# Layer 1 of a two-layer decoder: the order in which query and key stacks, weights, the last head and the memory's keys are worked

## The chip, the cores and the metric

One core of a Trainium2 chip. The metric is the device time of one execution of the whole program, in microseconds (us). The engines are TensorE (PE: matmuls; PEld: its weight loads), VectorE (DVE), ScalarE or Activation (ACT), GpSimd (POOL) and SyncE (SP, which issues most DMAs). Each runs its own instructions in order and waits for the others by semaphores.

## What is computed

A decoder of two layers over 1024 positions with 1024 features, in float32. Layer 0 has differential attention with 6 heads, layer 1 stick-breaking attention with 12 heads on keys and values that are projected once from the residual stream; both have a cross-attention into 256 memory tokens, a SiLU gate, an output projection and a residual addition. Layer 1, cut to what the change touches:

```python
h = rms_norm(x, b_norm[j]); proj = h @ b_w_in[j]
q, qm, gate = jnp.split(proj, [SB_W, SB_W + MEM_W], axis=-1)
# stick-breaking, per block of 128 queries
z = q @ k.T * scale
log_beta = log_sigmoid(z); log_1m = where(mask, log_sigmoid(-z), 0.0)
suffix = cumsum(log_1m, reverse=True) - log_1m
o = exp(where(mask, log_beta + suffix, -inf)) @ v
om = memory_attention(qm, mem, ...)
x = x + (concatenate([o, om]) * silu(gate)) @ b_w_out[j]
```

## The kernel before

Every float32 operand of a matmul is split into a high part, rounded by a cast to `F32R`, and a low part, the difference; a product is three matmuls (`mm3`: high x high, high x low, low x high). So each weight, each `h`, each query and key costs a cast (mostly on Activation) and a subtraction (on VectorE or POOL).

**Order.** TensorE's instructions run in the order in which the Python code emits them. The code builds lists of (cost, function) items; `mixed` and `merge` interleave a main list and a filling list in proportion to their costs, and `spread(a, b)` puts the items of `b` evenly behind the items of `a`. On the other engines and on SP a scheduler orders the instructions by its own estimate of when each can start and by the order in which they are emitted; `urgent()` sets an instruction 150 places further forward. So a change in the lists moves TensorE's work by hand and everything else by way of the scheduler.

**Pools.** PSUM has eight banks: `psc` 3 (scores), `ppj` 2 (all projections, tag `pj`), `ptr` 3 (transposes `tw`, `tb`, `ta`, the attention output `av`, tag `tr`). In SBUF, `wp` has 11 slots (split weights, reloaded outputs `ys`, residuals `res`), `rawp` 4 (weights as they land), `hp` 2 (the split `h` and the split layer output `yh` of one half of 512 tokens).

**Between the layers.** While the output projection of layer 0 for the second half of the tokens (`go1`, 64 items: 8 output blocks of 8) runs, the keys and values of the memory for layer 1 (`kv_products`, 8 items of 12 matmuls, L611 to L632) are merged in. `load_h` then makes `h` of the first half: `norms` (matmul `ms`, L232, then `r_t` on POOL by `rsqrt_pool`, L101), `rows` (L240) and eight urgent pieces. `km` is the memory's statistics, two splits (`prep`) and four turns of the keys (`turn`, matmul `ta`, L389). `plan1` does `norms`, `rows` and the pieces of the second half among the memory's query products `mp[b]` (eight of 8 items); their `nat` is turned by `turn_q` (`tb`, L378).

**A head in layer 1** (`StickUnit`, two of the 12 heads at a time, c = 0 and 1). `take_q` and `take_k` read a projection bank: Activation copies the high parts (L912, L913, L921), VectorE subtracts for the low parts. `S` makes scores, two sigmoids on Activation (L942, L943), a mask on POOL (L947), a scan (L949) and a product `be` on VectorE. `W` transposes `be` (`tw`, L531), splits it into `wT`, multiplies with the values (`av`, L971), and joins the halves: Activation copies `avt` (L980) and VectorE adds `y`. In `run_layer` step `n` has the scores of pair `n` and the `W` of the pair before; the projections of the next head and the gates fill in.

**Weights.** `load_turned` (L140) loads up to three blocks of 128 columns, `load_flat` (L158) one of 256. On the way "act" POOL scales the raw weight in place by the norm's gain, Activation casts it, POOL subtracts.

**The last head.** `out_proj(1, 0)` and `out_proj(1, 1)` give `load0`, `go0`, `load1`, `go1`: loads of the heads' outputs `y` from memory (`ys`, split to `yh`, L1017), and 64 items each, item (m, i) being block t = `order[i]` of output block m, with t = 5, the last head, at the end of each m. `tail` says what of them goes into which step of the last head (B = 48).

```python
items[0:2] = [items[0][:7], items[1][:7], items[0][7:], items[1][7:]]      # out_proj, l = 1, c = 0
tail = {B + 1: load0[:3], B + 2: load0[3:], B + 3: go0[:4], B + 4: go0[4:8] + load1[:3], ...
```

Of the kernel before, what the change touches and what calls it, by code (L numbers as in the profile page):

```python
# [8 lines left out]
F32 = mybir.dt.float32  # L9
F32R = mybir.dt.float32r  # L10
# [29 lines left out]
def trunk(ctx: ExitStack, tc: tile.TileContext, xT, memT, pos, gains, vecs, wA, wAm, wAg, wAo,  # L40
# [99 lines left out]
    def load_turned(ws, i, src, gbase, way="act"):  # L140
# [7 lines left out]
        r3 = raw.rearrange("p (k m) -> p k m", k=n)  # L148
        nc.sync.dma_start(r3, src[:, k0:k0 + n, :])
        tt(G, r3, r3, gn[:, gbase + k0:gbase + k0 + n].unsqueeze(2).broadcast_to([P, n, P]), ALU.mult)  # L150
        w = ws[i] = wp.tile([P, 2, 384], F32R, name="w", tag="w")
        S.copy(w[:, 0, :n * P], raw)  # L152
        tt(G, w[:, 1, :n * P], raw, w[:, 0, :n * P].bitcast(F32), ALU.subtract)
# [4 lines left out]
    def load_flat(ws, kt, src, gbase, st, way="act", last=None):  # L158
# [22 lines left out]
        if way == "vector":  # L181
            S.activation(hi, raw, AF.Copy, scale=g)
            V.scalar_tensor_tensor(lo, raw, g, hi.bitcast(F32), ALU.mult, ALU.subtract)
        else:
            G.tensor_scalar(raw, raw, g, 0.0, ALU.mult, ALU.add)
            S.copy(hi, raw)
            tt(G, lo, raw, hi.bitcast(F32), ALU.subtract)
# [707 lines left out]
    class StickUnit:  # L895
# [9 lines left out]
        def take_q(self, c, ps):  # L905
# [5 lines left out]
            for i, d in enumerate((LOW, HIGH)):  # L911
                S.copy(hi[i][d, :], ps[d, :])  # L912
                S.copy(hi[i][(HIGH, LOW)[i], :], ps[d, :])  # L913
                tt(V, lo[d, i, :], ps[d, :], hi[i][d, :].bitcast(F32), ALU.subtract)
            self.q[c] = hi, lo

        def take_k(self, c, ps):

            k = self.k[c] = kp.tile([P, 2, 512], F32R, name="k", tag="k")
            for i, d in enumerate((LOW, HIGH)):  # L920
                S.copy(k[d, i, :], ps[d, :])  # L921
                tt(V, k[(HIGH, LOW)[i], i, :], ps[d, :], k[d, i, :].bitcast(F32), ALU.subtract)

# [32 lines left out]
        def W(self, bc):  # L956
# [6 lines left out]
            def av(part, k0, k1):  # L963
# [15 lines left out]
                d, s_ = (lo, hi) if c == 0 else (hi, lo)  # L979
                S.copy(tmp[d, :], o[s_, :])  # L980
                tt(V, self.y[d, :], o[d, :], tmp[d, :], ALU.add)
                if c == 1:
# [4 lines left out]
    def value_chunks(p, ws, b):  # L987
# [17 lines left out]
        return [(C256, lambda kt=kt: go(kt)) for kt in range(8)]  # L1005


    def out_proj(l, c, wo):
# [20 lines left out]
        def go(m, i):  # L1029
# [12 lines left out]
            if i == 7:  # L1042
# [9 lines left out]
                else:  # L1052
                    nc.sync.dma_start(out[c, m], res)
        items = [[(C512, lambda m=m, i=i: go(m, i)) for i in range(8)] for m in range(8)]
        if l == 1 and c == 0:
            items[0:2] = [items[0][:7], items[1][:7], items[0][7:], items[1][7:]]
        return ([(0, lambda t=t: load(t)) for t in ((0, 2, 4) if l == 0 else order[:7])],
# [93 lines left out]
    def plan1(mem, hs, after):  # L1151
# [51 lines left out]
        add(-3, mp[0], norms1)  # L1203
        add(-2, mp[1][:7], rows1, p1, mp[1][7:])
        add(-1, spread(mp[2], load_g(7)))
        add(0, mp[3], gate(6, 0))
# [88 lines left out]
    def ends(l, wo):  # L1295
# [12 lines left out]
    first, lg, km, fills, ts, ss = plan1(mems[1], hs1, (n1, r1, p1))  # L1308
    merge(kv, go0 + d0 + go1[:4] + n0 + go1[4:9] + r0 + spread(go1[9:36], p0))
    merge([], spread(go1[36:44], km) + spread(go1[44:57], first + d1[:3]) + spread(go1[57:], lg) + d1[3:])  # L1310
    stick_mask()
    load0, go0 = out_proj(1, 0, wBo)
    load1, go1 = out_proj(1, 1, wBo)
    B = 8 * NH
    late = [(2000, lambda: None)]
    tail = {B + 1: load0[:3], B + 2: load0[3:], B + 3: go0[:4], B + 4: go0[4:8] + load1[:3], B + 5: go0[8:12] + load1[3:5],
            B + 6: go0[12:14] + late + go0[14:20], B + 7: go0[20:30] + load1[5:], B + 8: go0[30:41], B + 9: go0[41:49]}
    run_layer(1, mems[1], (fills, ts, ss), {}, tail)
    merge([], go0[49:] + go1)

# [66 lines left out]
```

## Time and profile before

| | us |
|---|---|
| median of 3 runs | 1349.86 (1347.27 to 1352.76) |
| the profiled execution | 1355.41 |
| its span, first to last instruction | 1353.7 |
| TensorE busy | 1263.8 (93%) |
| VectorE / Activation / POOL busy | 968.3 / 784.3 / 727.9 |
| mean granted TensorE clock | 0.978 |

Layer 0 takes the first 620 us or so, the passage between the layers ends near 745, the six head pairs of layer 1 follow at some 78 us each from 815 on, and the last 92 us are nearly all output projection. In the rows below, times are from the span's start; a group of instructions is given with its busy time, the mean of one in ns, and the idle time before it with what ended it; "busy (x)" is busy time and number of instructions; PEclk is the granted TensorE clock, 1.00 for 2.4 GHz and 0.50 for 1.2.

### The profile page before, as it was taken

To read this page: it belongs to the slowest core of one execution; us is meant where nothing else is said; L and a number is where in the kernel's file an instruction comes from. 1 tells how busy PE (TensorE), PEld (TensorE's weight loads), DVE (VectorE), ACT (ScalarE), POOL (GpSimd) and SP (SyncE) were. 2 spreads that over 40 slices of the span, in tenths; PEclk is the share of its full clock that TensorE was granted. 3 is DMA by queue.
4 is the path that set the end of the run, shared out by engine and by line. 5 is a ranking of instruction groups with operands and counts; after the bars stand their busy time and mean duration, and the time that the engine had idled before them with its cause. 6 is when DMAs were issued, how large, how long until landed. Compare 5 with 4: busy or idle time off the path is not lost.

```text
span 1353.7 us, 22630 instructions
## 1 busy us (share of the span) xinstructions
PE 1263.8 (93%) x7556; PEld 1126.8 (83%) x7556; DVE 968.3 (72%) x2211; ACT 784.3 (58%) x1986; POOL 727.9 (54%) x924
## 2 busy tenths in 40 slices
PE   7799999999999999999888999999899998988998
PEld 6688999898989888887777997789778897876787
DVE  8788777778787876775845645777767777898832
ACT  4566555555555656764645755666646665575631
POOL 7664544636462575945045755655655664455630
PEclk9899999999999999999989999999999999998999
DMA  5010110201011220357540142112120231222453
GB/s 213 24 49 27 39 36 22 58 9 53 23 47 32 74 78 28 124 179 245 176 129 24 34 134 67 45 48 93 52 67 28 75 94 55 69 72 86 131 165 117
DMA packets 75670, 105.65 MB, mean 78 GB/s; under 512 B 8353, under 2 KB 60321, under 8 KB 75297
## 3 DMA queue, kind: packets, MB, share of 16 engines
q1 hardware_dynamic: 75264, 104.05, 24.5%
q8 instruction: 60, 0.98, 0.3%
q14 instruction: 58, 0.47, 0.1%
q10 hardware_dynamic: 288, 0.15, 0.0%
HBM read 82.67 MB, written 21.50 MB: 77 GB/s over the span
## 4 chain that ended last, share of the span: by engine, by line
PE 64%; DVE 14%; POOL 6%; DMA 6%; ACT 5%; issue 5%; POOLq 0%; DVEq 0%; SPq 0%; ACTq 0%
PE pq L416 6%; PE pq L418 5%; PE pq L417 5%; PE tw L531 4%; PE pg L416 4%; PE pg L418 4%; PE pg L417 4%; PE sc L520 3%; PE sc L521 3%; DVE u L949 3%; PE av L971 3%; PE po L417 2%; PE po L416 2%; PE po L418 2%; PE tb L378 2%
## 5 line engine op out<-in xcount | busy, mean ns | idle before, releaser
L94 POOL TENSOR_TENSOR w<-raw,w 128x384 fp32r<-128x384 f32 (+1 forms) x182 | 195.3, 1082 | 32.2 <-ACT w L152 19.0
L416 PE MATMUL pq<-w,h 128*128 128x384 f32 (+1 forms) x448 | 162.0, 362 | 5.6 <-ACT h L223 5.3
L94 DVE TENSOR_TENSOR wT<-tw,wT 128x512 fp32r<-128x512 f32 (+2 forms) x248 | 138.6, 567 | 28.9 <-ACT wT L535 27.1
L949 DVE TENSOR_TENSOR_SCAN u<-u,stick 128x128 f32<-128x128 f32 (+3 forms) x96 | 133.9, 1395 | 32.6 <-ACT u L942 32.2
L418 PE MATMUL pq<-w,h 128*128 128x384 f32 (+1 forms) x448 | 149.7, 334 | 3.4 <-DVE h L224 3.2
L417 PE MATMUL pq<-w,h 128*128 128x384 f32 (+1 forms) x448 | 149.5, 334 | 0.2 <-POOL w L94 0.2
L535 ACT CAST wT<-tw 128x512 fp32r<-128x512 f32 (+2 forms) x248 | 122.3, 500 | 44.5 <-PE tw L531 41.9
L101 POOL TENSOR_TENSOR ss<-ss,mhalf 128x4 f32<-128x4 f32 x68 | 71.0, 1047 | 108.6 <-DVE ss L356 103.4
L947 POOL TENSOR_SCALAR_AFFINE_SELECT be<-be 128x128 f32<-128x128 f32 x96 | 79.0, 825 | 86.3 <-ACT be L943 84.3
L416 PE MATMUL pg<-h,w 128*128 128x512 f32 x256 | 109.4, 427 | 0.1
L818 ACT ACTIVATE e<-sc,nmd 128x512 f32<-128x512 f32 (+2 forms) x144 | 82.5, 579 | 42.9 <-DVE nmd L813 42.2
L416 PE MATMUL po<-yh,w 128*128 128x512 f32 x256 | 105.0, 410 | 2.0 <-DVE res L94 2.0
L418 PE MATMUL pg<-h,w 128*128 128x512 f32 x256 | 102.9, 402 | 1.3 <-POOL w L94 1.3
L417 PE MATMUL pg<-h,w 128*128 128x512 f32 x256 | 102.6, 401 | 0.0
L417 PE MATMUL po<-yh,w 128*128 128x512 f32 x256 | 102.0, 398 | 0.2 <-POOL yh L94 0.2
L94 DVE TENSOR_TENSOR be<-be,u 128x127 f32<-128x127 f32 (+3 forms) x96 | 88.7, 926 | 18.1 <-POOL be L947 13.3
L418 PE MATMUL po<-yh,w 128*128 128x512 f32 x256 | 101.6, 397 | 0.0
L531 PE MATMUL tw<-identR,be 128*128 128x128 f32 x432 | 75.0, 285 | 24.2 <-DVE y L94 12.9
L416 PEld LDWEIGHTS pq<-w,h 128*128 128x128 f32 x448 | 86.0, 192 | 8.4 <-POOL w L122 5.3
L418 PEld LDWEIGHTS pq<-w,h 128*128 128x128 f32 x448 | 85.7, 191 | 4.2 <-DVE h L224 4.2
L417 PEld LDWEIGHTS pq<-w,h 128*128 128x128 f32 x448 | 86.2, 192 | 3.5 <-POOL w L94 0.9
L531 PEld LDWEIGHTS tw<-identR,be 128*128 128x128 f32 x432 | 55.0, 146 | 36.2 <-DVE y L94 14.1
(237 smaller groups left out, 3931.4 us busy)
## 6 DMA issues: line engine op xcount, KB each, us to landing
raw<-in_wA_dram SPq DMA_DIRECT2D x44, 192.0 KB, 2.4
raw<-in_wAo_dram SPq DMA_DIRECT2D x32, 192.0 KB, 2.6
v_dr<-vs SPq DMA_DIRECT2D x48, 128.0 KB, 1.8
v<-v_dr SPq DMA_DIRECT2D x12, 512.0 KB, 3.5
raw<-in_wBo_dram SPq DMA_DIRECT2D x32, 192.0 KB, 2.5
raw<-in_wB_dram SPq DMA_DIRECT2D x36, 128.0 KB, 2.3
raw<-in_wB_dram SPq DMA_DIRECT2D x24, 192.0 KB, 2.4
wkv<-in_wM_dram SPq DMA_DIRECT2D x16, 256.0 KB, 3.1
```

Of the source, the lines that this page charges most:

```text
L94: eng.tensor_tensor(out_, a, b, op)
L101: G.tensor_tensor(t, t, mhalf[:, :n], ALU.pow)
L416: T.matmul(o, a[0], b[0], start=first, stop=False)
L417: T.matmul(o, a[0], b[1], start=False, stop=False)
L418: T.matmul(o, a[1], b[0], start=False, stop=last)
L520: T.matmul(sc[:, :m], qh, k[:, c, :m], start=True, stop=False)
L521: T.matmul(sc[:, :m], ql, k[:, c, :m], start=False, stop=True)
L531: T.transpose(t[:, j * P:(j + 1) * P], w[:, j * P:(j + 1) * P], identF)
L535: S.copy(hi, t3)
L818: S.activation(e[:, o:o + n], st["sc"][j], AF.Exp, bias=nm[:, 0:1], accum_out=st["l"][:, j, c:c + 1])
L947: G.affine_select(out=be[:, L - P:L], in_=be[:, L - P:L], pattern=[[-1, P]], compare_op=ALU.is_gt, fill=0.0, base=0, channel_multiplier=1)
L949: V.tensor_tensor_scan(u[:, 0:L][:, ::-1], u[:, 0:L][:, ::-1], keep["m"][:, 1024 - L:1024][:, ::-1], 1.0, ALU.mult, ALU.max)
```

## The change

1. `load_turned` and `load_flat`, way "act": Activation writes the high part itself with the gain as scale (up to three instructions of 128 columns, or one of 256), ahead of POOL's scaling in place; POOL's subtraction follows.
2. `take_q` and `take_k`: all of Activation's copies are emitted before VectorE's subtractions.
3. `StickUnit.W`: the copy `avt` and the addition `y` are urgent.
4. `out_proj(1, 0)`: the first three output blocks are summed over seven blocks of the input (without t = 5), and the sum is added into the residual at once; the last head's product for these three is done behind the fourth output block, from one more load of three weight blocks (`w5`), with a second addition and the store.
5. `plan1`: `rows` and the pieces of the second half come after three items of `mp[2]` instead of seven of `mp[1]`; the load of gate 7 stands alone.
6. Between the layers: four more items of `go1` before `norms`, six instead of five before `rows`, the pieces over 16 items instead of 27; the memory's statistics before six output items, its split and turns spread over the next 21 items among the loads of the memory's query weights.
7. The tail: output items from step B + 2 on and six more of them within the last head; the second half's loads at B + 8, B + 9 and after it, where they began at B + 4.

```diff
@@ load_turned, load_flat
+        w = ws[i] = wp.tile([P, 2, 384], F32R, name="w", tag="w")
+        for j in range(n):
+            S.activation(w[:, 0, j * P:(j + 1) * P], r3[:, j, :], AF.Copy, scale=gn[:, gbase + k0 + j:gbase + k0 + j + 1])
         tt(G, r3, r3, gn[:, gbase + k0:gbase + k0 + n].unsqueeze(2).broadcast_to([P, n, P]), ALU.mult)
-        w = ws[i] = wp.tile([P, 2, 384], F32R, name="w", tag="w")
-        S.copy(w[:, 0, :n * P], raw)
         tt(G, w[:, 1, :n * P], raw, w[:, 0, :n * P].bitcast(F32), ALU.subtract)
...
+            S.activation(hi, raw, AF.Copy, scale=g)
             G.tensor_scalar(raw, raw, g, 0.0, ALU.mult, ALU.add)
-            S.copy(hi, raw)
             tt(G, lo, raw, hi.bitcast(F32), ALU.subtract)
@@ take_q (take_k likewise)
                 S.copy(hi[i][d, :], ps[d, :])
                 S.copy(hi[i][(HIGH, LOW)[i], :], ps[d, :])
+            for i, d in enumerate((LOW, HIGH)):
                 tt(V, lo[d, i, :], ps[d, :], hi[i][d, :].bitcast(F32), ALU.subtract)
@@ StickUnit.W
-                S.copy(tmp[d, :], o[s_, :])
-                tt(V, self.y[d, :], o[d, :], tmp[d, :], ALU.add)
+                with urgent():
+                    S.copy(tmp[d, :], o[s_, :])
+                    tt(V, self.y[d, :], o[d, :], tmp[d, :], ALU.add)
@@ out_proj
+        def without(m, i):
+            if i == 0:
+                st["f", m] = load_packed(wo[m], way="act")
+                st["ps", m] = ppj.tile([P, 512], F32, name="po", tag="pj")
+                st["res", m] = wp.tile([P, 512], F32, name="res", tag="w")
+                nc.sync.dma_start(st["res", m], x1_dr[c][:, m, :])
+            f, yh, ps, t = st["f", m], y_split(l, c), st["ps", m], order[i]
+            mm3(ps, (f(0, t), f(1, t)), (yh[:, 0, t, :], yh[:, 1, t, :]), i == 0, i == 6)
+            if i == 6:
+                tt(V, st["res", m], ps, st["res", m], ALU.add)
+                if m == EARLY - 1:
+                    st["w5"] = load_w(wo[0:EARLY, :, order[7], :].rearrange("m p n -> p m n"), EARLY * P, way="act")
+        def last(m):
+            yh, w, t = y_split(l, c), st["w5"], order[7]
+            ps = ppj.tile([P, 512], F32, name="po", tag="pj")
+            o = slice(m * P, (m + 1) * P)
+            mm3(ps, (w[:, 0, o], w[:, 1, o]), (yh[:, 0, t, :], yh[:, 1, t, :]), True, True)
+            tt(V, st["res", m], ps, st["res", m], ALU.add)
+            nc.sync.dma_start(out[c, m], st["res", m])
...
-            items[0:2] = [items[0][:7], items[1][:7], items[0][7:], items[1][7:]]
+            items[:EARLY] = [[(C512, lambda m=m, i=i: without(m, i)) for i in range(7)] for m in range(EARLY)]
+            items[EARLY + 1:EARLY + 1] = [[(C512, lambda m=m: last(m)) for m in range(EARLY)]]
@@ plan1
-        add(-2, mp[1][:7], rows1, p1, mp[1][7:])
-        add(-1, spread(mp[2], load_g(7)))
+        add(-2, mp[1], mp[2][:3], rows1, p1, mp[2][3:])
+        add(-1, load_g(7))
@@ between the layers, and the tail
-    merge(kv, go0 + d0 + go1[:4] + n0 + go1[4:9] + r0 + spread(go1[9:36], p0))
-    merge([], spread(go1[36:44], km) + spread(go1[44:57], first + d1[:3]) + spread(go1[57:], lg) + d1[3:])
+    merge(kv, go0 + d0 + go1[:8] + n0 + go1[8:14] + r0 + spread(go1[14:30], p0))
+    merge([], km[:1] + go1[30:36] + spread(go1[36:44], km[1:2] + first[:2]) + spread(go1[44:57], km[2:] + first[2:] + d1[:3])
+          + spread(go1[57:], lg) + d1[3:])
...
-    late = [(2000, lambda: None)]
-    tail = {B + 1: load0[:3], B + 2: load0[3:], B + 3: go0[:4], B + 4: go0[4:8] + load1[:3], B + 5: go0[8:12] + load1[3:5],
-            B + 6: go0[12:14] + late + go0[14:20], B + 7: go0[20:30] + load1[5:], B + 8: go0[30:41], B + 9: go0[41:49]}
+    tail = {B + 1: load0[:2], B + 2: load0[2:4] + go0[:4], B + 3: load0[4:] + go0[4:10], B + 4: go0[10:16],
+            B + 5: go0[16:21], B + 6: go0[21:29], B + 7: go0[29:39], B + 8: go0[39:49] + load1[:2], B + 9: go0[49:55] + load1[2:5]}
...
-    merge([], go0[49:] + go1)
+    merge([], load1[5:] + go0[55:] + go1)
```

## Rows read from the trace of the kernel before

**Rows 1.** The page, part 1: busy us, share of span, instructions.

```profile
PE 1263.8 (93%) x7556; PEld 1126.8 (83%) x7556; DVE 968.3 (72%) x2211; ACT 784.3 (58%) x1986; POOL 727.9 (54%) x924
```

**Rows 2.** Busy by stretch: length, PE, PEld, DVE, ACT, POOL, PEclk, DMA, GB/s.

```profile
620.00:745.00 125.00, 107.37 (x592) 93.04 (x591) 75.23 (x152) 64.03 (x152) 50.06 (x64) 0.93 0.44 139
1206.00:1262.00 56.00, 43.35 (x220) 35.18 (x220) 47.89 (x64) 34.03 (x84) 31.43 (x36) 0.91 0.35 104
...
1306.00:1349.50 43.50, 43.50 (x193) 36.06 (x192) 13.69 (x26) 8.42 (x18) 0.00 (x0) 1.00 0.46 146
```

**Rows 3.** Waits of TensorE, whole run: total us, times, longest.

```profile
PE tw L531 <- DVE y L94: 12.9, 5, 3.2
PE tw L531 <- DVE be L94: 11.3, 9, 2.4
...
PE pq L416 <- DVE ql L94: 3.0, 2, 1.6
```

**Rows 4.** Groups of TensorE's instructions, 620 to 745 us; last column idle before.

```profile
L416 PE MATMUL pq<-wf,h 128*128 128x256 f32 x30 | 8.9, 296 | 1.4 <-DVE A L94 1.4
L378 PE MATMUL tb<-identR,nat 128*128 128x128 f32 x24 | 3.5, 273 | 4.7 <-POOL nat L94 3.1 <-ACT nat L367 1.6
...
L240 PE MATMUL rows<-identR,r_t 128*128 128x128 f32 x16 | 3.1, 358 | 3.2 <-POOL r_t L101 3.2
```

**Rows 5.** A head start in order of time; table of the stretch behind.

```profile
1132.26 1.60 DVE L94 TENSOR_TENSOR be<-be,u 128x1023 f32<-128x1023 f32 x1
...
1134.49 0.58 ACT L912 CAST qh<-pq 64x512 fp32r<-64x512 f32 x1 [2.16 <-DVE ql L94]
...
1136.42 0.42 DVE L94 TENSOR_TENSOR y<-av,avt 64x256 f32<-64x256 f32 x1
...
1136.89 0.66 PE L531 MATMUL tw<-identR,be 128*128 128x128 f32 x4 [2.48 <-DVE y L94]
...
1138.30:1141.70 3.40, 3.40 (x14) 3.04 (x13) 2.19 (x5) 1.20 (x3) 1.15 (x3) 0.50 0.00 0
```

**Rows 6.** Between the layers in order of time: start, us, instruction, idle before.

```profile
631.96 1.02 PE L232 MATMUL ms<-onesD,accs 128*128 128x1 f32 x8 [2.97 <-DVE accs L94]
...
648.14 0.42 DVE L94 TENSOR_TENSOR w<-wkv,w 128x256 fp32r<-128x256 f32 x1
...
649.27 0.28 PE L416 MATMUL pm<-w,hm 128*128 128x256 f32 x1
...
659.06 0.75 DVE L94 TENSOR_TENSOR w<-wkv,w 128x256 fp32r<-128x256 f32 x2
...
674.94 0.47 PE L389 MATMUL ta<-identR,nat 128*128 128x128 f32 x2 [4.70 <-DVE nat L94]
...
703.68 0.48 POOL L185 TENSOR_SCALAR raw<-raw,gn 128x256 f32<-128x256 f32 x1 [2.16 <-DMA raw<-in_wB_dram]
```

**Rows 7.** VectorE and POOL ahead of the `be` wait at 856.71.

```profile
853.99 2.57 DVE L94 TENSOR_TENSOR be<-be,u 128x511 f32<-128x511 f32 x1 [1.72 <-POOL be L947]
...
853.93 2.08 POOL L94 TENSOR_TENSOR wf<-raw,wf 128x256 fp32r<-128x256 f32 x3
```

**Rows 8.** Waits of TensorE from 1200 us to the end.

```profile
PE tw L531 <- DVE be L94: 4.6, 5, 2.1
```

**Rows 9.** Activation's groups in layer 1, and POOL's waits, 745 to 1200 us.

```profile
L152 ACT CAST w<-raw 128x384 fp32r<-128x384 f32 x40 | 20.9, 523 | 17.9 <-POOL raw L94 15.7 <-PE pq L418 1.3 <-PE pk L418 0.4
L186 ACT CAST wf<-raw 128x256 fp32r<-128x256 f32 x24 | 9.6, 421 | 4.9 <-POOL raw L185 2.7 <-PE pg L418 1.7
L943 ACT ACTIVATE be<-sc 128x128 f32<-128x128 f32 x24 | 7.0, 291 | 0.0
L182 ACT ACTIVATE wf<-raw,gn 128x256 fp32r<-128x256 f32 x6 | 3.0, 506 | 4.0 <-DMA raw<-in_wBm_dram 3.8 <-PE pm L418 0.2
...
POOL raw L94 <- DMA raw<-in_wB_dram: 18.1, 17, 2.3
POOL raw L185 <- DMA raw<-in_wB_dram: 10.5, 7, 2.0
```

More of the change, by code (lines that the diff above doesn't have):

```diff
@@ L921, in take_k @@
                 S.copy(k[d, i, :], ps[d, :])
+            for i, d in enumerate((LOW, HIGH)):
                 tt(V, k[(HIGH, LOW)[i], i, :], ps[d, :], k[d, i, :].bitcast(F32), ALU.subtract)
@@ L1005, in value_chunks @@
         return [(C256, lambda kt=kt: go(kt)) for kt in range(8)]
+    EARLY = 3
     def out_proj(l, c, wo):
```

## The prediction, made from these rows before the change was run

> **What bounds the kernel now.** I read first the busy times of the engines: TensorE is busy 1263.8 of 1353.7 us, VectorE 968, the others less [rows 1]. So the end is set by TensorE, and what a change is worth is what it takes from two things: the 90 us in which TensorE stands idle, and the stretches in which it runs at half its clock. The second view is the table by stage. In the stretch between the two layers the mean granted clock is 0.93, which is 0.07 x 125 = 8.7 us lost beside 17.6 us of idle; in the last head it is 0.91 (0.09 x 56 = 5.0 us) with 12.7 us idle, and VectorE is busy 47.9 of 56 us there [rows 2]. The third view names who ends TensorE's waits in the whole run: the addition that makes `y` (12.9 us in 5 waits), the product `be` (11.3 in 9), the low part of the query stack, `ql` (3.0 in 2) [rows 3]; and between the layers the low part of the memory's keys (4.7), the sums `accs` (3.0), `r_t` (3.2), the memory's queries `nat` (4.7) and `A` (1.4) [rows 4, 6].
>
> The fourth view is the order of time around one of the five `y` waits. Activation writes two of the four pieces of the query stack and stands for 2.16 us until VectorE has subtracted the first low half, because both read one PSUM bank. VectorE comes to that half only after its scan and its product. Then Activation's other two copies, its copy of `av`, VectorE's second low half and the `y` addition follow one another; TensorE needs the bank of `av` for its next transposes and waits 2.48 us [rows 5]. After that wait the granted clock is 0.50 for 3.4 us, so 1.7 us more are lost [rows 5]. The waits at 902, 980, 1059 and 1214 us look the same, each with a stretch at 1.2 GHz behind it.
>
> **The change part by part.** All terms are against the profiled execution, 1355.41 us (span 1353.7 and 1.7 around it).
>
> *Stacks engine by engine, and `av` urgent.* Activation's four copies then stand together (4 x 0.58 = 2.3 us) and nothing of VectorE lies between them; `avt` can follow 0.4 us after `av` is done, and `y` (0.42 us) comes ahead of the low halves in VectorE's queue. At the wait at 1136.89 the product `be` ends at 1133.86, so `y` could be done near 1134.3, and TensorE, whose wait began 2.48 us before, arrives at 1134.4 [rows 5]. Next late is then the bank of the transposes before, which needs their copy and subtraction, about 1 us later than `y` and behind 0.7 us of matmuls. So of 12.9 + 5 x 1.7 = 21.4 us I take 17.5; 0.4 us may stay at each place, and at one a stretch at half clock. The low end is 9: the first low half now waits for all four copies, and if `be` or a transpose bank takes over half of each wait, part of the stretches stays. The query is needed some 40 us later, so late low halves hold only the projection bank; that bank's waits on `ql` (3.0 us, [rows 3]) go, I take 2.5, between 0 and 3.
>
> *Between the layers, first half.* `norms` comes four output items later in TensorE's order. An item is three matmuls; in the last 43.5 us of the run 64 of them follow one another [rows 2], 0.68 us each, so 2.7 us of work fill the wait for `accs`: 3.0 us and its half-clock stretch of 1.7. The first turn of the memory's keys stood four output items behind the end of the first merge and stands fifteen behind it now: 11 items of 0.68 us are 7.5 us, where TensorE waited 4.7 for the keys' `nat` [rows 6]. So 4.7 us and the two half-clock stretches behind it (3.4) go; of the 8.7 us of clock in this stage [rows 2] these three are 5.1. Together 12.8. But TensorE then comes earlier, and the memory's weights may not: they were ready at 648.56 and used at 649.27, 0.7 us of slack [rows 6], and the change packs their products closer. If the last of them stayed where it was (659.81, [rows 6]), the 1.4 us of products and 38 items of 0.68 us behind it would end this part at 687.1 and, with 1.1 us of turns, at 688.2; in the trace it ended at 694.8, so 6.6 are left. I take 8.5, nearer the low end, because that slack is the nearest row.
>
> *Between the layers, second half.* `rows` comes after four more memory items (4 x 0.36 = 1.4 us), and all of the second memory product stands ahead of the eight urgent pieces of `h`, so its evacuation no longer queues behind their 10 us on VectorE. That removes the waits on `A` and `nat` (1.4 + 4.7 + one stretch 1.7) and 1.4 of the 3.2 us on `r_t`. Against it: `r_t` was late since POOL stood in front of it for 2.16 us waiting for a weight to land [rows 6], and an earlier TensorE meets the same landings. Of 12.7 us (1.4 + 4.7 + 3.2 + two stretches) I take 5, between 0 and 12.7.
>
> *The last head.* Beside its `y` wait, counted above, it has 9.3 us of waits (five on `be` make 4.6 [rows 8]) and two stretches of 1.7: 12.7 us. Taken away: seven `yh` subtractions of the second half in the thick of it, some 0.8 us each; they go behind the scans' end, and their loads, which held weight slots, with them. 28 instead of 14 output items can now run before the last head is needed. Added: three more VectorE additions at 0.69 us, one load of 192 KB with its cast (0.5) and POOL subtraction (1.3), and three output tiles that hold weight slots longer. I take 5.5, between -3 (the additions land in VectorE's queue ahead of the products) and 12.7.
>
> *Weights scaled on Activation.* A turned weight took one copy of 384 columns, 523 ns [rows 9]; now it takes three scaled ones of 128. The trace has no such copy. A plain 128-wide one is 291 ns, and scaling by a column costs 506 - 421 = 85 ns [rows 9], so about 376 each; consecutive ones overlap by some 0.1, which gives 0.93 for three: 0.41 us more for each of the 40, 0.24 for each of the 20 two-wide ones, 21 us of Activation over 600 us. It is covered as long as Activation has idle time there (it is busy 58%, [rows 1]). The landing waits of POOL (18.1 + 10.5 = 28.6 us in 24 waits between 745 and 1200 us, [rows 9]) become Activation's, and behind Activation are queued the copies `wT` and `avt` that TensorE waits for. Bounds 0 and -50; I take -4, nearer to nothing, since in that stretch TensorE waits for Activation almost never, and -10 is the end I keep in the range.
>
> *The flat weights' order.* Two of the `be` waits (2.4 and 2.35 us and one stretch: 6.4) stand beside POOL's three subtractions in a row: the product of 511 columns took 2.57 us, while POOL worked 2.08 [rows 7]; the mean of the twelve is 1.2. Scale and subtraction now follow one another on POOL, so I expect pairs and not triples; I take 2, between 0 and 6.4. What the row shows is that VectorE stood until the whole series was over. The Trainium skill ("SBUF — State Buffer", section "SBUF: two separate sides") has it that whichever of the two engines starts first holds the pair for one whole instruction and the other fully blocks; by that rule VectorE would get in after the first 0.7 us, and this trace disagrees for a series. By the rule the term would be 4 and the sum 2 us better.
>
> Sum: 17.5 + 2.5 + 8.5 + 5 + 5.5 + 2 - 4 = 37. 1355.4 - 37 = 1318.4. The profiled run is 5.5 us above the median of three (1349.86), so **1313 us**.
>
> **The rivals.** (a) *The waits move.* Once the bank is free in time, `be` ends the same waits (it is already the second releaser), and between the layers the landings set the pace: 9 + 2.5 + 6.6 + 0 - 1 + 0 - 4 = 13, which is 1337. For it: VectorE's 47.9 of 56 us in the last head, and the 0.7 us of slack. Against it: at the head starts `be` had ended 3 us before TensorE went on. Chance 0.20. (b) *The change doesn't do what it says.* The order on Activation, VectorE and POOL is made by a scheduler that weighs its own times; if it puts `y` and the copies where they were, only the order on TensorE, which is written by hand, changes: 6.6 - 4 = 2.6, which is 1347. Chance 0.08. (c) *Slower: Activation stands for weights.* Activation works in order. If each of the 24 landing waits (28.6 us) and the 21 us of added copies reached TensorE, 50 us would stand against 41 gained: 1355.4 + 9 - 5.5 = 1359. It decides from about 48 of the 50 us on, so nearly all of them would have to lie in front of a copy TensorE needs; Activation's 42% of idle time speaks against it. Chance 0.06 (it takes in other ways of the same kind, such as a copy of `avt` that stands in front of a late `av`).
>
> **How the numbers follow.** The forecast has 0.62, (a) 0.20, (b) 0.08, (c) 0.06, and 0.04 stay for better than 1294, where the second to fifth terms come near their upper ends (a gain of 56). The range is 1294 to 1338: from there to the value of (a), which is the sum of the low ends; it leaves out about 0.20. A measurement of this kernel can tell about 0.5% from no change, so 1343.1 and 1356.6 are the bounds: faster 0.62 + 0.04 + 0.19 of (a) = 0.85, within 0.5% 0.09 ((b) and the edge of (a)), slower 0.06.
>
> **What would show it.** Head starts: four `qh` copies without a gap, `y` within 1 us of `avt`, TensorE's waits on `y` under 3 us in sum, and no stretch of 0.50 at 903, 981, 1060 and 1138. Between the layers: no wait on `accs` or on the keys' `nat` over 1 us, and a mean clock of 0.96 or more; a new wait of `pm` on `w` would show the landings. In the last head: TensorE's idle time about half. Activation's scaled copies of 128: near 376 ns. I am wrong if TensorE's waits on `be` grow by more than 8 us, or if waits on `wT` that Activation is late with sum to more than 10.

## The result, and the profile after

The changed kernel takes 1328.09 us (median; runs of 1326.3, 1327.21 and 1328.97), the kernel before 1350.41 beside it: ratio 0.9832, 95% interval 0.9803 to 0.986, so 22.7 us gained by the ratio. The forecast was 1313 and a gain of 37; the range, 1294 to 1338, holds the time. One execution of 1520.1 us, whose granted clock was 0.75 from end to end, is left out, and the profile below is that of a further run of the same kernel (1329.92 us, span 1328.1, mean granted clock 0.981).

The page, part 1, and the table by stretch: the passage between the layers, two stretches of the last head (the second with its last waits), and the stretch behind one head start. Columns as in [rows 1, 2].

```profile
PE 1255.5 (95%) x7556; PEld 1121.6 (84%) x7556; DVE 975.4 (73%) x2214; ACT 810.6 (61%) x2087; POOL 740.6 (56%) x925
```

```profile
620.00:745.00 125.00, 115.46 (x676) 99.25 (x675) 81.00 (x166) 74.03 (x185) 57.58 (x71) 0.99 0.47 145
1181.00:1237.00 56.00, 48.98 (x263) 41.33 (x262) 47.52 (x65) 34.78 (x84) 36.30 (x41) 0.94 0.28 87
1237.00:1277.00 40.00, 33.01 (x176) 28.00 (x177) 31.02 (x33) 22.06 (x48) 24.02 (x21) 0.91 0.49 154
1109.60:1116.40 6.80, 5.98 (x21) 5.26 (x22) 4.73 (x10) 1.74 (x4) 1.80 (x3) 0.50 0.07 20
```

Against [rows 2] the passage gave what was hoped: TensorE's idle time there fell from 17.6 to 9.5 us, and the clock rose from 0.93 to 0.99, another 7.5. The window is fixed, so after the change it holds more of what follows the passage (676 matmuls where it held 592), and its clock varies by itself: kernels of the sets below that leave the order of this passage as it was show 0.90 to 0.95. The last head did not: 7.0 us idle in the first stretch and 7.0 in the second, at clocks of 0.94 and 0.91.

TensorE's waits, whole run (total, times, longest):

```profile
PE tw L532 <- DVE y L94: 20.4, 7, 6.9
...
PE po L417 <- ACT w L124: 3.3, 1, 3.3
PE tw L532 <- DVE be L94: 2.5, 1, 2.5
```

Against [rows 3] the waits on `ql` are gone and those on `be` fell from 11.3 to 2.5; those on `y`, which the largest term of the sum was to remove, grew from 12.9 to 20.4. A wait of `po` on a weight is new. Groups of the passage (620 to 745 us):

```profile
L418 PE MATMUL pm<-w,hm 128*128 128x256 f32 x32 | 9.1, 286 | 1.5 <-DVE w L94 1.5
...
L379 PE MATMUL tb<-identR,nat 128*128 128x128 f32 x32 | 3.7, 240 | 0.2 <-POOL nat L94 0.2
...
L233 PE MATMUL ms<-onesD,accs 128*128 128x1 f32 x16 | 1.9, 240 | 0.0
```

Of the waits of [rows 4, 6] on `A` (1.4), `nat` (4.7 twice) and `accs` (3.0) 0.5 us are left: `ms` and `pq` have none, `tb` 0.2 and the gates 0.3 on `A`. Of the 3.2 on `r_t` 1.8 are left. The landings show as 1.5 us of `pm` on `w`, and as the 3.3 of `po` on `w`.

A head start in order of time, the place of [rows 5]:

```profile
1103.70 0.58 ACT L913 CAST qh<-pq 64x512 fp32r<-64x512 f32 x1 [0.85 <-PE pq L419]
...
1106.83 1.78 DVE L94 TENSOR_TENSOR be<-be,u 128x1023 f32<-128x1023 f32 x1
1106.86 0.36 ACT L984 COPY avt<-av 64x256 f32<-64x256 f32 x1
...
1108.54 1.38 DVE L94 TENSOR_TENSOR ql<-pq,qh 64x512 fp32r<-64x512 f32 x2
...
1109.95 0.42 DVE L94 TENSOR_TENSOR y<-av,avt 64x256 f32<-64x256 f32 x1
...
1110.42 1.12 PE L532 MATMUL tw<-identR,be 128*128 128x128 f32 x4 [2.93 <-DVE y L94]
```

Activation does what was forecast: four copies without a gap (the first is shown, the last ends at 1106.06), `avt` done at 1107.22. But on VectorE `y` still stands behind both low halves `ql`, 1.38 us, and comes 2.7 us behind `avt`. The product `be` in front of them is late too: it ends at 1108.6, 1.1 us after TensorE came to its wait (1110.42 less 2.93); in [rows 5] it had ended half a microsecond before. The stretch at 0.50 behind this wait is the last line of the table above.

Activation's copies of weights, and the waits for landing weights that are left, 745 to 1200 us:

```profile
L152 ACT ACTIVATE w<-raw,gn 128x128 fp32r<-128x128 f32 x144 | 47.2, 399 | 12.2 <-PE pk L419 4.9 <-DMA raw<-in_wBg_dram 3.5 <-PE pq L419 2.9
L186 ACT ACTIVATE wf<-raw,gn 128x256 fp32r<-128x256 f32 x18 | 9.0, 512 | 3.6 <-PE pg L419 1.7 <-DMA raw<-in_wB_dram 1.5
```

A scaled copy takes 399 ns (376 estimated). GpSimd's waits for landing weights [rows 9], 33.2 us with those for the gates, are gone, and 5.0 us of such waits are Activation's: most of them did not move, they ended. GpSimd still scales and subtracts each weight, and it waits for Activation's copies as long as before (16.4 us, 17.2 before).

### The profile page after: what moved, and what is told of

It is laid out like the page before. It is cut to its first block, busy times and chain, and to the rows that moved or that the text cites. A ratio compares the mean times of both kernels' runs of the same rounds, so it can differ in the third digit from the quotient of the medians.

```text
span 1518.3 us, 22822 instructions
## 1 busy us (share of the span) xinstructions
PE 1486.0 (98%) x7556; PEld 1249.9 (82%) x7556; DVE 967.0 (64%) x2214; ACT 821.8 (54%) x2087; POOL 733.3 (48%) x925
## 4 chain that ended last, share of the span: by engine, by line
PE 91%; DVE 4%; ACT 2%; POOL 1%; issue 1%; DMA 1%; POOLq 0%; DVEq 0%
PE pq L417 8%; PE pq L418 8%; PE pq L419 8%; PE tw L532 7%; PE po L417 5%; PE po L419 5%; PE po L418 5%; PE pg L418 4%; PE pg L417 4%; PE av L974 4%; PE pg L419 4%; PE sc L521 4%; PE sc L522 4%; PE pv L417 2%; PE pv L418 2%; PE pk L419 2%
## 5 line engine op out<-in xcount | busy, mean ns | idle before, releaser
L417 PE MATMUL pq<-w,h 128*128 128x384 f32 (+1 forms) x448 | 180.7, 403 | 5.4 <-ACT h L224 5.4
L419 PE MATMUL pq<-w,h 128*128 128x384 f32 (+1 forms) x448 | 171.0, 382 | 4.1 <-DVE h L225 4.1
L952 DVE TENSOR_TENSOR_SCAN u<-u,stick 128x128 f32<-128x128 f32 (+3 forms) x96 | 139.9, 1457 | 49.5 <-ACT u L945 48.5
L418 PE MATMUL pq<-w,h 128*128 128x384 f32 (+1 forms) x448 | 169.9, 379 | 0.2 <-POOL w L94 0.2
L950 POOL TENSOR_SCALAR_AFFINE_SELECT be<-be 128x128 f32<-128x128 f32 x96 | 99.1, 1032 | 119.8 <-ACT be L946 114.8
L417 PE MATMUL pg<-h,w 128*128 128x512 f32 x256 | 122.2, 477 | 0.0
L417 PE MATMUL po<-yh,w 128*128 128x512 f32 x256 | 120.4, 470 | 0.0
L419 PE MATMUL pg<-h,w 128*128 128x512 f32 x256 | 118.0, 461 | 0.0
L418 PE MATMUL pg<-h,w 128*128 128x512 f32 x256 | 116.9, 457 | 0.0
L418 PE MATMUL po<-yh,w 128*128 128x512 f32 x256 | 116.6, 455 | 0.0
L419 PE MATMUL po<-yh,w 128*128 128x512 f32 x256 | 116.0, 453 | 0.0
L417 PEld LDWEIGHTS pq<-w,h 128*128 128x128 f32 x448 | 94.1, 210 | 12.2 <-POOL w L122 5.3
L418 PEld LDWEIGHTS pq<-w,h 128*128 128x128 f32 x448 | 95.2, 212 | 7.1 <-POOL w L94 0.6
L419 PEld LDWEIGHTS pq<-w,h 128*128 128x128 f32 x448 | 92.5, 207 | 8.7 <-DVE h L225 5.2
L974 PEld LDWEIGHTS av<-wT,v 128*128 128x128 f32 x480 | 81.5, 205 | 15.9
L532 PE MATMUL tw<-identR,be 128*128 128x128 f32 x432 | 85.4, 315 | 6.1 <-DVE y L94 4.5
L945 ACT ACTIVATE u<-sc 128x128 f32<-128x128 f32 (+3 forms) x144 | 71.3, 495 | 34.8 <-PE sc L522 30.2
```

The lines of the kernel that those rows point to most:

```text
L417: T.matmul(o, a[0], b[0], start=first, stop=False)
L418: T.matmul(o, a[0], b[1], start=False, stop=False)
L419: T.matmul(o, a[1], b[0], start=False, stop=last)
L532: T.transpose(t[:, j * P:(j + 1) * P], w[:, j * P:(j + 1) * P], identF)
L945: S.activation(u[:, o:o + n], sc, AF.Sigmoid, scale=-0.125)
L950: G.affine_select(out=be[:, L - P:L], in_=be[:, L - P:L], pattern=[[-1, P]], compare_op=ALU.is_gt, fill=0.0, base=0, channel_multiplier=1)
```

## The experiments

Every ratio is to the kernel before, run on the same chip in the same set; its medians were 1351.75, 1352.29 and 1353.12 us in the three sets below. Gains are (1 - ratio) times that median. The changed kernel was timed in its own set only, but for one execution in the first set, so a difference from it is one of two ratios, each with its interval. A profile is of one execution, which can lie several us from the median of its kernel (6.6 in scale_heads, 6.2 in tail_alone): waits are read from it, gains from the medians.

### First set: parts of the change

**no_scale**: the change without its part 1.

```diff
-        for j in range(n):
-            S.activation(w[:, 0, j * P:(j + 1) * P], r3[:, j, :], AF.Copy, scale=gn[...])
         tt(G, r3, r3, gn[...], ALU.mult)
+        S.copy(w[:, 0, :n * P], raw)
...          # load_flat likewise
```

> The changed kernel without its first part: weights are scaled on POOL and cast on Activation as before. Theory A (the forecast's small term, 4 us): 4 us faster than the changed kernel, about 1324. Theory B (the missing 15 us are Activation standing for weights and copying in more pieces): about 1313. Theory C (scaling on Activation is a gain, since POOL no longer waits between its two steps): 1330 or more.

Measured: 1342.63, ratio 0.9945 (0.9925 to 0.9965). The changed kernel's ratio is 0.0113 lower, so the scaling on Activation is a gain of some 15 us beside the other parts (10 to 20 with both intervals), as theory C had it; the term of -4 has the wrong sign.

**heads**: the kernel before with parts 2 and 3 alone (stacks engine by engine; `avt` and `y` urgent).

> The kernel before with the stacks written engine by engine and av urgent, nothing else. The forecast's terms: 17.5 + 2.5 = 20 us faster than before, about 1330, with waits on y under 3 us and no stretch at half clock at the head starts. Rival (the waits move to be and the transposes' banks): 11.5 us, about 1339, with be waits up by 8 us.

Measured: 1352.66, ratio 1.0008 (0.9987 to 1.0029): nothing, and both theories fall. TensorE's waits between 745 and 1200 us, in the kernel before and in heads:

```profile
PE tw L531 <- DVE y L94: 9.6, 4, 2.6
```

```profile
PE tw L531 <- DVE y L94: 8.7, 4, 2.6
...
PE pv L416 <- DVE k L94: 4.5, 2, 2.3
```

The waits on `y` are where they were, with both low halves in front of `y` at each head start. Those on `ql` are gone, and a new one has come: of `pv` on the low halves of the keys. The prediction had worked out the query stack alone, but `take_k` was changed in the same way.

**between**: the kernel before with parts 5 and 6 alone.

> The kernel before with the new order between the layers alone (output items before the norms, the keys' turns spread, the second half's pieces later). The forecast's terms: 8.5 + 5 = 13.5 us faster, about 1337. If the memory's weights set the pace: 6.6 us or less, 1344 or more, with new waits of pm on w or of pq on wf. At the upper ends: 25 us, 1325.

Measured: 1339.96, ratio 0.992 (0.9891 to 0.9949), 10.8 us gained (6.9 to 14.7). As forecast (13.5), though the new wait of the rival came in kind: `po` waits 2.9 us for `w`.

### Second set: what the scaling and the order of `y` are worth

**scale_alone**: the kernel before with part 1 alone.

> The kernel before with one part of the change only: Activation scales the turned and flat weights while it casts them. Theory A (GpSimd's landing waits are what the old way costs: GpSimd stands for a weight while a mask of layer 1 queues behind it, so the product be, the scan's follower on VectorE, comes late; the other edits are not needed for that): about 9 us gained, 1342 (1338 to 1345), GpSimd's waits for landing weights between 745 and 1200 us fall from 33 us to under 5, VectorE's waits on the mask from 13 to about 8. Theory B (the gain shows only beside the stacks written engine by engine, whose late key halves it covers): 1349 or more. The prediction on record (the copies cost Activation 21 us and TensorE 4): 1355.

Measured: 1346.81, ratio 0.9964 (0.9942 to 0.9986): 4.9 us (1.9 to 7.8). Between the two theories, and against the prediction. GpSimd's waits for landing weights went as theory A had it, and VectorE's waits on the mask fell from 13.3 to 7.4 us.

**touch**: the changed kernel, with the landing wait put back on GpSimd.

```diff
         nc.sync.dma_start(r3, src[:, k0:k0 + n, :])
+        G.tensor_scalar(seen, raw[:, :1], 1.0, 0.0, ALU.mult, ALU.add)
...          # load_flat likewise
```

> The changed kernel with one small instruction added ahead of Activation's scaled copies: GpSimd reads one column of each landed weight into a scratch column, so that GpSimd waits for the landing again, and everything else stays as in the change (72 copies of 128 x 1, an instruction of the size of the shortest GpSimd rows, some 0.1 us each). Theory A (the landing wait in front of the masks is the cost that the scaling on Activation took away): back to the time without the scaling, 1340 to 1344, waits on the mask on VectorE near 20 us between 745 and 1200, the waits of pv on k back. Theory B (the gain comes from GpSimd's new order of scale and subtraction, or from Activation's copies being free of GpSimd): 1328 to 1333.

Measured: 1333.47, ratio 0.9875 (0.9841 to 0.9908), some 6 us worse than the change by the ratios, with intervals that overlap, so it may be nothing. GpSimd's waits, 745 to 1200 us:

```profile
POOL seen L151 <- DMA raw<-in_wB_dram: 31.1, 20, 2.5
...
POOL seen L188 <- DMA raw<-in_wB_dram: 8.7, 10, 1.3
POOL seen L151 <- DMA raw<-in_wBg_dram: 7.8, 6, 2.6
```

47.6 us of landing waits are on GpSimd again, about as many as in no_scale (50.2), and VectorE waits 27.4 us for masks, more than in no_scale (20.2). But the waits of `pv` on `k` came back with 0.8 us of 4.5, and the time is nearer theory B. So the landing wait is at most some 6 of the 15 us, and the added instructions themselves (84 in all, mostly 0.19 us each) are in these 6. Why the rest does not come back is not shown; GpSimd's new order of scale and subtraction is what touch leaves in place.

**y_first**: the changed kernel, with the low halves of both query stacks queued on VectorE behind the next `y` (an ordering edge, no wait).

```diff
+            def low():
                 for i, d in enumerate((LOW, HIGH)):
                     tt(V, lo[d, i, :], ps[d, :], hi[i][d, :].bitcast(F32), ALU.subtract)
+            if self.h > 0:
+                StickUnit.held.append(low)
+            else:
+                low()
...
-                    tt(V, self.y[d, :], o[d, :], tmp[d, :], ALU.add)
+                    yi = V.tensor_tensor(self.y[d, :], o[d, :], tmp[d, :], ALU.add)
+                with tc.issue_after(yi.ins):
+                    self.flush()
```

> The changed kernel with the low halves of the query stacks of heads 1 to 5 queued on VectorE behind the next addition y. Theory A (the urgent mark did not move y: the two low halves, 1.38 us, stand ahead of it at every head start): the y waits of 2.9 us at two heads fall to about 1.5, those of 0.5 vanish, that of 5.7 falls to 4.3: 5.2 us, and up to 5 of half-clock stretches, 1324 (1320 to 1326). Theory B (what ends these waits is the long product be in front of both, or the banks of the transposes, which come due right behind): 1327 or more, and TensorE waits as long, on wT or be instead of y.

Measured: 1334.44, ratio 0.9865 (0.9821 to 0.9908): not better. TensorE's waits:

```profile
PE tw L532 <- DVE y L1000: 13.6, 7, 6.9
PE pq L417 <- DVE ql L94: 7.7, 5, 2.5
```

A head has two query stacks, some 17 us apart. Behind the second the wait on `y` went, and 0.7 us on `wT` stands there; the first one's bank was now held too long, and `pq` waited for it, at 953 and 1103 us (2.5 and 2.1) with a half-clock stretch. The waits on `y` that are left are those of the last head (4.8, 1.0 and 6.9). The expectation's size was wrong since it did not tell the two apart.

**y_first_late**: the same, and in the last head the low halves `yh` stand behind `y` (the last three of the first half, all seven of the second, whose loads are emitted behind the last head's steps for it).

> The same, and in the last head the low halves of the loaded outputs yh are queued behind y as well: the last three of the first half of the tokens behind the y of the head start, all seven of the second half behind the last y but one. Theory A: the y waits of 5.7 and 6.9 us fall to 1.5 and to about 2.5, some 8 us against the changed kernel in these two places beside the 5 to 10 of the first heads: 1315 (1311 to 1320). Theory B (the output products then wait for yh, whose seven subtractions of 0.7 us stand between y and the first item of the second half): 1322 or more, with waits of po on yh of over 3 us behind the last head.

Measured: 1328.76, ratio 0.9835 (0.9803 to 0.9867): 4.1 us better than y_first by the ratios, where some 8 were expected, with intervals that overlap. The two waits on `y` fell to 1.6 and 1.7 us as expected; behind them `tw` now waits 2.9 us for `wT`, and `po` 1.2 for `yh`.

### Third set: the parts together, and better orders

**scale_heads**: the kernel before with parts 1, 2 and 3.

> The kernel before with three parts of the change: Activation scales the weights, the stacks are written engine by engine, avt and y are urgent. Alone the first gained 4.9 us and the other two together nothing. Theory A (the parts lean on each other: stacks written engine by engine put both low halves of the keys behind GpSimd's work on the weights, the waits of pv on k of 2.3 us and their half-clock stretches, and the scaling takes these away again): more than the sum, 13 to 15 us gained, 1337, no wait of pv on k over 0.5 us. Theory B (the parts add up): 1347, and the 14 us between the changed kernel and the one without scaling come from the passage and the last head.

Measured: 1338.34, ratio 0.9885 (0.9854 to 0.9917): 15.6 us, where the parts alone gave 4.9 and nothing. Theory A. What the scaling takes away is seen at one place in no_scale and in the changed kernel. First no_scale:

```profile
904.50 0.83 POOL L94 TENSOR_TENSOR raw<-raw,gn 128x384 f32<-128x384 f32 x1 [2.23 <-DMA raw<-in_wBg_dram]
...
904.76 0.38 ACT L945 ACTIVATE be<-sc 128x256 f32<-128x256 f32 x1
...
907.46 0.54 POOL L949 TENSOR_SCALAR_AFFINE_SELECT be<-be 128x128 f32<-128x128 f32 x2
...
907.79 1.50 DVE L94 TENSOR_TENSOR be<-be,u 128x127 f32<-128x127 f32 x2 [1.91 <-POOL be L949]
...
909.31 1.39 DVE L94 TENSOR_TENSOR k<-pk,k 64x512 fp32r<-64x512 f32 x2
...
910.85 0.36 PE L416 MATMUL pv<-wf,h 128*128 128x256 f32 x1 [2.26 <-DVE k L94]
```

Then the changed kernel:

```profile
896.44 0.83 POOL L94 TENSOR_TENSOR raw<-raw,gn 128x384 f32<-128x384 f32 x1 [0.23 <-ACT w L152]
...
897.11 0.40 ACT L946 ACTIVATE be<-sc 128x256 f32<-128x256 f32 x1
897.22 0.42 POOL L950 TENSOR_SCALAR_AFFINE_SELECT be<-be 128x128 f32<-128x128 f32 x1
...
898.57 0.68 POOL L950 TENSOR_SCALAR_AFFINE_SELECT be<-be 128x128 f32<-128x128 f32 x1
...
899.43 1.39 DVE L94 TENSOR_TENSOR k<-pk,k 64x512 fp32r<-64x512 f32 x2
...
900.96 0.35 PE L417 MATMUL pv<-wf,h 128*128 128x256 f32 x1
```

Without the scaling GpSimd comes to the masks of two `be` 2.3 us after the later one is ready, since weights and other work stand in front of them; VectorE waits 1.91 for the masks, the keys' low halves queue behind that, and TensorE waits 2.26 us for the bank of `pk`. With it one mask is made between GpSimd's two steps on a weight and the other right behind them, 1.1 us after its `be` is ready, and TensorE goes on. There are two such places in no_scale, each with a stretch at half clock that loses 1.7 us, some 8 us together; two `y` waits of 1.8 us went to 0.5, and two waits on `be` of 1.2 us went. scale_heads has no wait of `pv` on `k` either.

**tail_alone**: the kernel before with parts 4 and 7.

> The kernel before with the last part of the change only: the first three output blocks without the last head's block and the new order of loads and items in the last head. Theory A (by the sum of the other parts, 11.8 and 14 of the 22.3 us gained, this part gives back what its later loads cost: the yh subtractions now stand ahead of the last y on VectorE and TensorE waits 6.9 us there): 0 to 4 us slower, 1352 to 1356. Theory B (the prediction's term): 5.5 us faster, 1346.

Measured: 1352.76, ratio 0.9993 (0.9974 to 1.0011): nothing. TensorE's waits:

```profile
PE tw L531 <- DVE y L94: 22.3, 7, 6.9
```

Those on `be` and `res` in the last head went as forecast, and the same time came back as waits on `y`: 4.6 us at the start of the last head (3.2 before), 1.0 within it and 6.9 at its end.

**y_second**: as y_first, but only the second stack's low halves are held back.

```diff
-            if self.h > 0:
+            if c == 1 and self.h > 0:
```

> The changed kernel with the low halves of the second query stack of heads 1 to 5 alone queued on VectorE behind y; the first stack's stay where they are, since holding them back cost waits of pq on ql of 1.0 and 2.5 us. Theory A (the wait at a head start is that order on VectorE, which the prediction took to be reversed): the y waits of 2.9 us at two heads fall to 0.7 on wT, with the half-clock stretch behind the second, that of 5.7 to 4.8: about 7 us, 1321 (1318 to 1325). Theory B (VectorE is full around a head start, so any order gives a wait of the same size elsewhere): 1327 to 1331.

Measured: 1324.69, ratio 0.9789 (0.9768 to 0.9811), 5.8 us better than the change by the ratios (1 to 10.6 with both intervals, which just overlap). Theory A: the two waits of 2.9 us became 1.45 and 1.49, and `wT`, the next late, takes 0.67 behind them. TensorE's waits:

```profile
PE tw L532 <- DVE y L1000: 15.9, 7, 6.9
...
PE tw L532 <- DVE wT L94: 3.2, 5, 0.7
```

On `y` and `wT` together that is 19.1 us, 1.3 less than the 20.4 on `y` in the changed kernel. More is in the stretch at half clock behind the wait at 1110.42, which loses 3.4 us: in the profile of y_second the clock is 1.00 there. So theory B has a part in it: of each of the two waits of 2.9 us 2.1 stay, on the late `be` and then on `wT`.

**best**: y_second, `yh` behind `y`, and the last output block's weights of layer 0 loaded eight items earlier.

```diff
-          + spread(go1[44:57], km[2:] + first[2:] + d1[:3])
+          + go1[44:48] + [(0, lambda: x1_st[1]["weights"](7))] + spread(go1[48:57], km[2:] + first[2:] + d1[:3])
...
+    def behind(i, f):
+        with tc.issue_after(StickUnit.ys[i]):
+            f()
...          # tail: the last three of load0 through behind(-1, ...), load1 out of steps B + 8 and B + 9
-    merge([], load1[5:] + go0[55:] + go1)
+    merge([], [(0, lambda f=f: behind(-2, f)) for _, f in load1] + go0[55:] + go1)
```

> As y_second, and two more edits: in the last head the low halves of the loaded outputs yh stand behind y, as in y_first_late; and between the layers the weights of the last output block are loaded eight items earlier, ahead of the memory's query weights, which held the four landing slots in front of them. Theory A: the wait of po on w at 686 us (3.3 and a half-clock stretch of 1.7) goes, some 5 us; the last head gives 3 to 5; with y_second's 7 in all 15 us against the changed kernel: 1313 (1309 to 1319). Theory B (earlier output weights make the memory's query weights late by as much, and yh is then waited for): within 3 us of y_second, with new waits of pq on wf of over 2 us between 695 and 715 us.

Measured: 1318.94, ratio 0.9752 (0.9728 to 0.9776): 33.6 us faster than the kernel before, 10.8 than the change and 5 than y_second (there the intervals just overlap). TensorE's waits, and VectorE near the end of the last head:

```profile
PE tw L532 <- DVE y L1000: 7.4, 7, 1.6
...
PE tw L532 <- DVE wT L94: 6.7, 7, 2.9
```

```profile
1253.58 0.41 DVE L1000 TENSOR_TENSOR y<-av,avt 64x256 f32<-64x256 f32 x1
1253.91 3.68 DVE L94 TENSOR_TENSOR yh<-ys,yh 128x512 fp32r<-128x512 f32 x6
```

The waits on `y` are 7.4 us in sum and the wait of `po` on `w` is gone. Short of the 1313 expected: the six `yh` now stand in front of `wT` (2.9 us), `po` waits 1.2 us for `yh`, and `ms` 2.1 us for `accs` at 693.6.

## Why the prediction was right or wrong

**Right: between the layers.** Forecast 13.5 us in two terms, measured 10.8 alone. The waits on `accs`, the keys' `nat`, `A` and the queries' `nat` were taken away; that on `r_t` fell from 3.2 to 1.8 us in the change, by as much as forecast (in between it stayed at 3.2). The price, slack of landing weights, came, though chiefly at another place than named: not `pm` on `w` (1.5 us) but `po` on `w` (3.3, and 1.7 lost at half clock behind it), because the memory's query weights took the landing slots ahead of the last output block's. The run best, which loads that block ahead of them, no longer has the wait.

**Wrong: the stacks and `av` urgent, 17.5 us.** The failed step is that `y` "comes ahead of the low halves in VectorE's queue". It doesn't: the scheduler put `y` behind both of them at the second stack of every head, and the urgent mark did not change it. Alone the term was worth nothing (heads). With the order made as the step assumed it, y_second gains 5.8 us more, a third of the term, so the order was not the only fault: the sum took `be` to be done before TensorE comes, and in the changed kernel it ends 1.1 us after, which is the move of the waits that rival (a) names. Rival (b), that the order stays, was right for this part, and had been weighed for the change as a whole only. A third fault: the keys' stacks were not costed. Their two waits in heads, 4.5 us and 1.7 lost at half clock behind the first, are about what the waits on `ql` (3.0, gone as forecast) and others gave back: between 745 and 1200 us TensorE's waits sum to 20.6 us before and 20.7 in heads. Query stacks, key stacks and the urgent mark were not run apart, so what each alone is worth is not shown.

**Wrong sign: the weights scaled on Activation and the flat weights' order, -4 and 2.** Both are part 1, measured as 4.9 alone and some 15 beside the others. The added work was right: 47.2 + 9.0 us where the copies of turned weights (384 and 256 columns) and of flat ones took 18.9 + 7.5 + 7.2 in that stretch before, 22.6 more. So was the flat order, though too small: the two waits on `be` and their stretch (6.4 us) are gone in scale_alone and in the change, and between 820 and 1200 us the mean product of 511 columns fell from 1.24 us to 0.69, since GpSimd's three subtractions no longer stand in a row [rows 7] (some products of 255 columns now stand beside a subtraction, and their mean rose from 0.42 to 0.65):

```profile
843.56 1.46 POOL L187 TENSOR_SCALAR raw<-raw,gn 128x256 f32<-128x256 f32 x2
843.61 0.69 DVE L94 TENSOR_TENSOR be<-be,u 128x511 f32<-128x511 f32 x1 [0.85 <-POOL be L950]
...
844.99 0.74 POOL L94 TENSOR_TENSOR wf<-raw,wf 128x256 fp32r<-128x256 f32 x1
```

So alone the rest of part 1 cost about 1.5 us by the difference, with an interval of 3 us either way, so the -4 is not refuted there. Beside the other parts the failed step is "The landing waits of POOL ... become Activation's": they fell from 33.2 to 5.0 us, and the prediction had not asked what queues behind GpSimd in the old order. It is the masks, for which the chain from `be` to `k` to `pv` waits once the stacks are written engine by engine; the other 10 us come with that (scale_heads against scale_alone and heads). Rival (c) is far off. How much of it is the landing wait and how much GpSimd's other order isn't settled: touch gives at most some 6 us to the first, and perhaps nothing. Nor are late masks a cost everywhere: touch has more waits on them than no_scale and nearly none of the keys' waits, so they seem to matter only where they stand ahead of the keys' low halves; no run tests that alone.

**Wrong: the last head, 5.5 us.** Measured 0.9 alone, which is nothing within its interval. The failed step is that the seven subtractions of the second half "go behind the scans' end". VectorE behind the last scan, in the changed kernel, and TensorE's wait:

```profile
1260.32 1.42 DVE L94 TENSOR_TENSOR yh<-ys,yh 128x512 fp32r<-128x512 f32 x1
...
1262.26 0.88 DVE L94 TENSOR_TENSOR yh<-ys,yh 128x512 fp32r<-128x512 f32 x1
...
1264.73 1.48 DVE L94 TENSOR_TENSOR yh<-ys,yh 128x512 fp32r<-128x512 f32 x1
1266.13 0.41 DVE L94 TENSOR_TENSOR y<-av,avt 64x256 f32<-64x256 f32 x1
...
1266.59 1.11 PE L532 MATMUL tw<-identR,be 128*128 128x128 f32 x4 [6.86 <-DVE y L94]
```

Three of the seven stand between the last scan and `y`, the other four ahead of it, around the scan before. The loads were moved in TensorE's order only; VectorE's order is the scheduler's, and it put the subtractions where their data was ready. That is the same fault as with `y`. Behind `y` (y_first_late, best) they seem to cost less but stand in front of `wT`: VectorE, busy 47.5 of the 56 us from 1181 on, leaves little room for any order there.

**That the time came within the range is luck in part**, since the faults partly cancel: 20 + 5.5 forecast for the stacks with `ql` and for the last head were worth about nothing, and -2 for part 1 was worth up to 15. The parts as measured, 15.6 for the first three, 10.8 and 0.9, make 27 where the whole gained 22.7; with an interval of about 4 us either way on most of them they agree. Nor is the upper end of the range what the prediction calls it: the low ends that it gives add up to a gain of 2.6 us and not to the 13 of (a).

## What to carry to other kernels

A mark that lets an instruction go earlier is a wish; an order between two instructions of one engine that a gain depends on has to be made as an edge, and read in the order of the built program. Where a step moves to another engine, ask what queues behind that step on the engine that stood waiting in the old chain: here the masks behind GpSimd's work on the weights were worth more than the added 22 us on Activation. And of a helper changed in two callers, cost both: the second stack of a head wanted `y` first, the first one did not, and the keys' stacks lost what the queries' won. And once a wait's last cause is put off, look at what was done just before it: half a microsecond of slack on `be` had become 1.1 us of lateness.

## What the runs showed of the chip

VectorE's products and GpSimd's work on weights hold one another up, and which of them waits differs by instruction. GpSimd's subtraction of two tensors held VectorE: in the changed kernel the product of 255 columns takes 0.42 us at 893.49 and 1.24 at 900.85, beside a subtraction of 1.01 that is recorded 0.05 us ahead of it. GpSimd's scaling by a column (TENSOR_SCALAR), recorded 0.06 us ahead, did not: at 862.42 the product of 767 columns takes 0.96 us, as it does with no neighbour, and the scaling beside it 1.28 instead of the 0.48 that one takes alone ([rows 6] show such a one). In the fence further above, two scalings beside the product of 511 columns take 1.46 together, so there too it was GpSimd that waited.

```profile
893.49 0.42 DVE L94 TENSOR_TENSOR be<-be,u 128x255 f32<-128x255 f32 x1
...
900.80 1.01 POOL L94 TENSOR_TENSOR w<-raw,w 128x384 fp32r<-128x384 f32 x1
900.85 1.24 DVE L94 TENSOR_TENSOR be<-be,u 128x255 f32<-128x255 f32 x1
```

```profile
862.36 1.28 POOL L187 TENSOR_SCALAR raw<-raw,gn 128x256 f32<-128x256 f32 x1
862.42 0.96 DVE L94 TENSOR_TENSOR be<-be,u 128x767 f32<-128x767 f32 x1 [0.24 <-POOL be L950]
```

The Trainium skill ("SBUF — State Buffer", section "SBUF: two separate sides") has it that of a VectorE instruction with two inputs in SBUF and a GpSimd instruction that reads SBUF the one that starts first holds the shared ports for the whole instruction, and the other is blocked. For one subtraction the trace agrees as recorded; for a series [rows 7] it does not, since VectorE got in behind the third only. For the scaling it does not as recorded either, but starts 0.06 us apart can't settle which engine was first.

Nor is each wait followed by half a clock: behind the wait of 2.93 us at 1110.42 the granted clock was 0.50 for 6.8 us, behind one of 2.90 at 964.15 it stayed at 1.00. A sum that adds a stretch to every wait has a spread of its own.

```profile
964.10:967.50 3.40, 3.35 (x22) 3.01 (x23) 3.15 (x7) 1.74 (x4) 0.56 (x3) 1.00 0.14 39
```
